# Input differences of a feed-forward made under the products ahead of it, with output blocks in the order 0 4 1 5 2 6 3 7

## Chip, cores and metric

The kernel runs on one core of a Trainium2 chip. The metric is the device time of one execution in microseconds (us). The engines are TensorE (PE, its weight loads apart as PEld), VectorE (DVE), ScalarE (ACT), GpSimd (POOL) and SyncE (SP), which issues most transfers.

## What is computed

Two layers of a decoder trunk on one sequence of 512 positions and 1024 channels, in float32. The feed-forward (FFN) width is 2816, and the mixer is a stick-breaking attention (4 heads) beside a Mamba2 scan (24 heads), both gated and merged into one output projection.

```python
def swiglu(h, w_up, w_down):
    gate, up = jnp.split(h @ w_up, 2, axis=-1)
    return (jax.nn.silu(gate) * up) @ w_down

def reference(...):
    for l in range(DEPTH):                                   # DEPTH = 2
        x = x + 0.5 * swiglu(rms_norm(x, ffn1_norm[l]), ffn1_w_up[l], ffn1_w_down[l])
        h = rms_norm(x, mix_norm[l])
        proj = h @ w_in[l]
        ...                                                  # attention, scan, their projections
        merged = jax.nn.sigmoid(gate_sb) * y_sb + jax.nn.sigmoid(gate_ssm) * y_ssm
        x = x + merged @ w_out[l]
        x = x + 0.5 * swiglu(rms_norm(x, ffn2_norm[l]), ffn2_w_up[l], ffn2_w_down[l])
    return rms_norm(x, final_norm)
```

## The kernel before

**Layout and precision.** The activations lie with channels on partitions: `x` is eight tiles of 128 channels by 512 positions, "blocks" 0 to 7. Every product is made three times with split operands (`mm3`, L291 to L293): high weight by high input, low weight by high input, high weight by low input. The high half is a copy rounded to the matmul's format, the low half the difference.

**Weight units.** The weights come as a fixed list of units of 128x1024 (`unit_order`). SP loads a unit into `wraw` (three buffers), ACT casts it to `whi` (L258), DVE subtracts to get `wlo` (L260); `ahead` starts a unit's conversion two units before its product. A dense unit is 24 matmuls of 512 columns. In the FFNs only the first blocks of gate and up are dense (`pairs_from`: four blocks in the first FFN, two elsewhere). The others go in pairs (`pair_of_blocks`): seven parts, 11, 12, s2, s1, s3, s4 and 22, each 24 matmuls of 256 columns, stand for the four dense units of two blocks. The s parts take sums of weights (`s`, by accumulating transfers from POOL's queue and an add on DVE) and, as inputs, differences of the halves of blocks k and k+4.

**Input differences.** `combine` makes them, pair after pair of blocks: two ACT copies with the gain (L354, L355), a DVE step (L357), a POOL subtraction (L358), two DVE steps (L360, L361), two ACT casts `th` (L364), and two subtractions for the low halves (L368), one on POOL and one on DVE. It starts when the FFN starts, and part s2 of the first pair needs all four. It scales by the gain alone; the norm's factor `rs` is multiplied in later, on the products.

**Norm ahead of an FFN.** As each block of `x` is finished (by the mixer's eight out products or the last slice's down products), `x_final` makes its high and low halves (`hhi` on ACT L478, `hlo` on DVE L480), its square (ACT L491) and adds that to `acc` (L498, on POOL except for block 7). `norm_end` sums over partitions with a matmul (L506) and forms `rs` (L514 to L516).

**Order.** Each engine runs its instructions in the order of the code. The code of a product calls `tick` once for each block k, and each tick lets every spawned generator (a conversion, a gate, `combine`, a norm) go one step. So an ACT or DVE step of `combine` stands among the conversions according to its ticks. FFN slices are blocks 0 to 7, 8 to 15 and 16 to 21; each ends with eight down products. The first FFN's beginning (`opening`) makes two units together as the input arrives.

Of the kernel before, what the change touches and what calls it, by code (L numbers as in the profile page):

```python
# [87 lines left out]
def pairs_from(layer, f):  # L88

    return 4 if (layer, f) == (0, 1) else 2  # L90


def unit_order(layer):

    def ffn(f):
# [29 lines left out]
    for m in range(KB):  # L125
        yield (layer, "out", m), KB
# [13 lines left out]
class Builder:  # L140
# [203 lines left out]
    def combine(self, gain):  # L344


        nc, half = self.nc, SEQ // 2
        a, b = slice(0, half), slice(half, SEQ)
        while len(self.h) < KB:
            yield 1  # L350
        for k in range(KB // 2):
            m = k + KB // 2
            u, v, x = self.tt[k], self.tt[m], self.x[k]
            nc.scalar.activation(u[:, b], x[:, b], AF.Copy, scale=gain[:, k:k + 1])  # L354
            nc.scalar.activation(v, self.x[m], AF.Copy, scale=gain[:, m:m + 1])  # L355
            yield 2
            nc.vector.scalar_tensor_tensor(u[:, a], x[:, a], gain[:, k:k + 1], u[:, b], op0=ALU.mult, op1=ALU.subtract)  # L357
            nc.gpsimd.tensor_tensor(u[:, b], v[:, b], u[:, b], op=ALU.subtract)  # L358
            yield 1
            nc.vector.scalar_tensor_tensor(v[:, b], u[:, a], -1.0, v[:, b], op0=ALU.mult, op1=ALU.subtract)  # L360
            nc.vector.scalar_tensor_tensor(v[:, a], v[:, b], -1.0, v[:, a], op0=ALU.mult, op1=ALU.subtract)  # L361
            yield 1
            for i in (k, m):
                nc.scalar.copy(self.th[i], self.tt[i])  # L364
                yield 1
            for i, eng in ((k, nc.gpsimd), (m, nc.vector)):
                lo = self.t(self.tp, [P, SEQ], "tt", F32R)
                eng.tensor_tensor(lo, self.tt[i], self.th[i].bitcast(F32), op=ALU.subtract)  # L368
                self.diff[i] = (self.th[i], lo)
            yield 1  # L370
            self.combined = k + 1
# [102 lines left out]
    def norm_split(self, m, gain):
# [6 lines left out]
        self.h.append((hi, lo))  # L481

    def norm_square(self, m, last=False):
# [13 lines left out]
        eng = nc.gpsimd if self.pos > 8 and m < KB - 1 else nc.vector  # L497
        eng.tensor_tensor(self.acc, self.acc, sq, op=ALU.add)  # L498
# [149 lines left out]
    def ffn(self, layer, f, gain, gain_next):  # L648
        tc = self.tc
        with tc.tile_pool(name=f"act{layer}{f}", bufs=8, reuse_waits="tile") as ap, \  # L650
                tc.tile_pool(name=f"ffn{layer}{f}", bufs=3, reuse_waits="tile") as fp, \
                tc.tile_pool(name=f"sx{layer}{f}", bufs=2, reuse_waits="tile") as self.sx, \
                tc.tile_pool(name=f"tt{layer}{f}", bufs=KB + 2, reuse_waits="tile") as tp:
            self.gated = {}
            self.th = [self.t(tp, [P, SEQ], "th", F32R, bufs=KB) for _ in range(KB)]
            tiles = [None] * KB
            for k in range(KB // 2):
                tiles[k], tiles[k + KB // 2] = (self.t(tp, [P, SEQ], "tt") for _ in range(2))
            self.tp, self.diff = tp, [None] * KB
            self.tt, self.combined = tiles, 0  # L660
            if self.pos:
                self.spawn(self.combine(gain))
            for s, (j0, j1) in enumerate(SLICES):
                act = []
                last = s == len(SLICES) - 1
# [19 lines left out]
                for m in range(2):  # L685
                    both.append((self.t(self.pmm, [P, SEQ], "mm"), self.unit(layer, f, "down", s, m, ahead=m == 0)))
                    self.dense(*both[m], act, 0, n - 2, stop=False)
                for m in range(KB):
                    if m < 2:
                        if m:  # L690
# [412 lines left out]
    def mixer(self, layer):  # L1103
# [13 lines left out]
        with ExitStack() as mix:  # L1117
            enter = mix.enter_context
            self.yo = enter(tc.tile_pool(name=f"yo{layer}", bufs=SBH, reuse_waits="tile"))
            self.yt = enter(tc.tile_pool(name=f"yt{layer}", bufs=24, reuse_waits="tile"))  # L1120
# [83 lines left out]

    def build(self):
# [145 lines left out]
```

## Time and profile before

| | |
|---|---|
| median of 3 runs | 2638.4 us (2638.17 to 2638.59) |
| the profiled execution's own time | 2638.81 us |
| its span in the profile | 2637.1 us |
| its mean granted TensorE clock | 0.995 |
| PE busy | 2598.7 us, 15072 matmuls |
| DVE busy | 1766.3 us, 2291 instructions |
| ACT busy | 1305.0 us, 2100 instructions |
| POOL busy | 603.3 us, 700 instructions |

Times on a timeline are counted from the span's start. A granted clock of 1 is 2.4 GHz, 0.5 is 1.2 GHz. Matmuls overlap, so a stretch of PE is measured from start to start. The four places where an FFN starts its first pair are near 57 us (layer 0's first), 990 (its second), 1339 and 2295 (layer 1's).

### The profile page before, as it was taken

How to read it: one execution, taken by the hardware profiler on the slowest of the kernel's cores; microseconds unless marked ns; L12 is line 12 of the kernel's file. 1: busy time of each engine (PE TensorE's matmuls, PEld its weight loads, DVE VectorE, ACT ScalarE, POOL GpSimd, SP SyncE). 2: the span in 40 equal slices, each digit the busy share in tenths (PEclk: the TensorE clock that was granted, in tenths of full speed). 3: DMA queues.
4: the chain of work that ended last, by engine and by line, in shares of the span. 5: the costliest groups of instructions: out<-in, count | busy, mean ns of one | idle time of the engine just before them, and what ended most of it. 6: DMA issues, size and time to landing. Idle time of an engine off the chain costs nothing.

```text
span 2637.1 us, 38181 instructions
## 1 busy us (share of the span) xinstructions
PE 2598.7 (99%) x15072; PEld 2296.3 (87%) x15072; DVE 1766.3 (67%) x2291; ACT 1305.0 (49%) x2100; POOL 603.3 (23%) x700
## 2 busy tenths in 40 slices
PE   8999999999999999999999999999999999999997
PEld 6999988888888889899988989888888888899996
DVE  7676775565665468585785858766666744785765
ACT  6443456655554245353553535566555543543444
POOL 2121211133232023021240212112332410321212
PEclk9999999999999999999999999999999999999999
DMA  5555442333333445463454644423333244374642
GB/s 177 160 144 152 119 138 74 103 105 105 115 92 127 138 136 156 135 183 112 142 141 139 168 124 133 131 75 113 96 116 104 97 136 160 89 185 130 177 123 74
DMA packets 103284, 337.94 MB, mean 128 GB/s; under 512 B 12048, under 2 KB 13328, under 8 KB 103104
## 3 DMA queue, kind: packets, MB, share of 16 engines
q1 hardware_dynamic: 91584, 294.53, 35.1%
q0 software_dynamic: 11232, 40.90, 8.7%
q8 instruction: 118, 1.93, 0.3%
q14 instruction: 62, 0.51, 0.1%
q10 hardware_dynamic: 288, 0.07, 0.0%
HBM read 322.77 MB, written 12.68 MB: 127 GB/s over the span
## 4 chain that ended last, share of the span: by engine, by line
PE 89%; DVE 6%; ACT 2%; issue 1%; POOL 1%; DMA 1%; ACTq 0%; DVEq 0%; SPq 0%; POOLq 0%
PE mm L291 25%; PE mm L293 24%; PE mm L292 24%; PE pa L293 3%; PE pa L292 3%; PE pa L291 3%; DVE wlo L260 1%; PE pa L1005 1%; PE pt L768 1%; PE pa L842 1%; PE pa L1007 1%; PE pt L990 1%; PE pt L988 1%; ACT whi L258 1%; DVE cv L906 0%
## 5 line engine op out<-in xcount | busy, mean ns | idle before, releaser
L258 ACT CAST whi<-wraw 128x1024 fp32r<-128x1024 f32 (+2 forms) x433 | 433.2, 1000 | 598.8 <-PE mm L293 497.5
L260 DVE TENSOR_TENSOR wlo<-wraw,whi 128x1024 fp32r<-128x1024 f32 (+2 forms) x433 | 572.8, 1323 | 161.4 <-ACT whi L258 160.0
L291 PE MATMUL mm<-hhi,whi 128*128 128x512 f32 (+1 forms) x1840 | 674.0, 366 | 1.9 <-ACT th L364 1.1
L292 PE MATMUL mm<-hhi,wlo 128*128 128x512 f32 (+1 forms) x1840 | 653.8, 355 | 14.5 <-DVE wlo L260 14.5
L293 PE MATMUL mm<-hlo,whi 128*128 128x512 f32 (+1 forms) x1840 | 654.7, 356 | 0.0
L292 PEld LDWEIGHTS mm<-hhi,wlo 128*128 128x128 f32 x1840 | 350.9, 191 | 59.0 <-DVE wlo L260 16.4
L293 PEld LDWEIGHTS mm<-hlo,whi 128*128 128x128 f32 x1840 | 350.2, 190 | 50.3 <-DVE hlo L480 0.3
L291 PEld LDWEIGHTS mm<-hhi,whi 128*128 128x128 f32 x1840 | 350.4, 190 | 44.0 <-ACT th L364 1.4
L601 POOL TENSOR_TENSOR g<-g,rs 128x512 f32<-128x512 f32 x78 | 137.5, 1763 | 729.8 <-DVE g L608 710.1
L260 DVE TENSOR_TENSOR wlo<-s,whi 128x1024 fp32r<-128x1024 f32 x156 | 242.1, 1568 | 53.9 <-ACT whi L258 53.9
L291 PE MATMUL mm<-act,whi 128*128 128x512 f32 x704 | 274.0, 389 | 0.0
L292 PE MATMUL mm<-act,wlo 128*128 128x512 f32 x704 | 274.0, 389 | 0.0
L293 PE MATMUL mm<-act,whi 128*128 128x512 f32 x704 | 273.9, 389 | 0.0
L292 PE MATMUL mm<-th,wlo 128*128 128x256 f32 x936 | 265.3, 283 | 1.2 <-DVE wlo L260 1.2
L291 PE MATMUL mm<-th,whi 128*128 128x256 f32 x936 | 265.1, 283 | 0.4 <-ACT g L606 0.4
L293 PE MATMUL mm<-tt,whi 128*128 128x256 f32 x936 | 265.0, 283 | 0.0
L627 DVE SCALAR_TENSOR_TENSOR x<-mm,x 128x512 f32<-128x512 f32 x96 | 66.1, 688 | 208.5 <-PE mm L293 208.5
L258 ACT CAST whi<-s 128x1024 fp32r<-128x1024 f32 x156 | 163.1, 1046 | 85.8 <-PE mm L293 46.2
L292 PEld LDWEIGHTS mm<-th,wlo 128*128 128x128 f32 x936 | 179.8, 192 | 1.8 <-DVE wlo L260 1.8
L291 PEld LDWEIGHTS mm<-th,whi 128*128 128x128 f32 x936 | 180.0, 192 | 0.6 <-ACT g L606 0.6
L293 PEld LDWEIGHTS mm<-tt,whi 128*128 128x128 f32 x936 | 179.8, 192 | 0.0
L906 DVE SCALAR_TENSOR_TENSOR cv<-mm,conv,cv 128x511 f32<-128x511 f32 (+2 forms) x192 | 142.4, 743 | 24.6 <-ACT cv L903 22.8
(258 smaller groups left out, 4630.6 us busy)
## 6 DMA issues: line engine op xcount, KB each, us to landing
wraw<-in_wflat_dram SPq DMA_DIRECT2D x353, 512.0 KB, 3.7
s<-in_wflat_dram SPq DMA_DIRECT2D x78, 512.0 KB, 5.0
s<-in_wflat_dram POOLq DMA_DIRECT2D x78, 512.0 KB, 9.1
wraw<-in_wflat_dram SPq DMA_DIRECT2D x64, 384.0 KB, 3.1
cumb<-cum_d SPq DMA_DIRECT2D x16, 768.0 KB, 4.1
xd<-x SPq DMA_DIRECT2D x16, 256.0 KB, 4.1
wraw<-in_wflat_dram SPq DMA_DIRECT2D x16, 256.0 KB, 3.3
x<-xd SPq DMA_DIRECT2D x16, 256.0 KB, 4.2
```

What stands on the lines that cost most here:

```text
L258: nc.scalar.copy(hi[:, :n], raw[:, :n])
L260: nc.vector.tensor_tensor(lo[:, :n], raw[:, :n], hi[:, :n].bitcast(F32), op=ALU.subtract)
L291: mm(ps, a[0], b[0], start=start, stop=False, **kw)
L292: mm(ps, a[1], b[0], start=False, stop=False, **kw)
L293: mm(ps, a[0], b[1], start=False, stop=stop, **kw)
L601: eng.tensor_tensor(r, r, self.rs[:, cols].unsqueeze(1).to_broadcast([P, 2, half]), op=ALU.mult)
L627: self.nc.vector.scalar_tensor_tensor(x, pd, 0.5, x, op0=ALU.mult, op1=ALU.add)
L768: self.nc.tensor.transpose(pt[:, cs], src[:, cs], self.ident)
L842: nc.tensor.matmul(pz[:, (i - j) * P:n], lhs, part, start=False, stop=(i == j and part is sps[i][1]), skip_group_check=True)
L906: nc.vector.scalar_tensor_tensor(u[:, i:], ps[:, :SEQ - i], tap[KCONV - 1 - i], u[:, i:], op0=ALU.mult, op1=ALU.add)
L988: nc.tensor.matmul(pc[:, :P], bt[:, span(c)], ct[:, span(c)], start=True, stop=True)
L990: nc.tensor.matmul(pu, btok[:, c, :], xws[c].rearrange("p h d -> p (h d)"), start=True, stop=True)
```

## The change

`combine` now makes one pair of blocks (k, k+4) and is spawned by `x_final` as soon as block k+4 has its `hlo`: during the mixer's out products for the second FFN, and during the last down products of a second FFN for the next layer's first. Out and down products go in the order 0 4 1 5 2 6 3 7. In the opening, the four are spawned 10, 19, 28 and 37 ticks after the first units. All of `combine`'s POOL steps go to DVE, and so does every `acc` addition (36 of them leave POOL). The first FFN keeps six dense blocks in place of four: one pair less. The tiles of `combine` move to a pool of their own beside `x`, which is opened with `x` at the mixer's out products; `yo` and `yt`, tiles of the mixer's branches, share that room and are closed before. Since the first out product comes behind this opening, the reloads of `x` are issued behind the mixer's last branch product.

```diff
+OUT_ORDER = tuple(i // 2 + KB // 2 * (i % 2) for i in range(KB))
...
-    return 4 if (layer, f) == (0, 1) else 2
+    return 6 if (layer, f) == (0, 1) else 2
...
-            for m in range(KB):
+            for m in OUT_ORDER:
                 yield (layer, f, "down", s, m), j1 - j0
...
-    def combine(self, gain):
...
-        while len(self.h) < KB:
-            yield 1
-        for k in range(KB // 2):
...
-            nc.gpsimd.tensor_tensor(u[:, b], v[:, b], u[:, b], op=ALU.subtract)
...
-            for i, eng in ((k, nc.gpsimd), (m, nc.vector)):
...
+    def combine(self, k, gain):
...
+        u, v = (self.t(self.tp, [P, SEQ], "uv", bufs=2) for _ in range(2))
+        nc.scalar.activation(u[:, b], x[:, b], AF.Copy, scale=gain[:, k:k + 1])
+        nc.scalar.activation(v, self.x[m], AF.Copy, scale=gain[:, m:m + 1])
+        yield 2
+        nc.vector.scalar_tensor_tensor(u[:, a], x[:, a], gain[:, k:k + 1], u[:, b], op0=ALU.mult, op1=ALU.subtract)
+        nc.vector.tensor_tensor(u[:, b], v[:, b], u[:, b], op=ALU.subtract)
+        yield 1
...
+        for t in (u, v):
+            two.append(self.t(self.tp, [P, SEQ], "th", F32R, bufs=KB))
+            nc.scalar.copy(two[-1], t)
             yield 2
...
-        eng = nc.gpsimd if self.pos > 8 and m < KB - 1 else nc.vector
-        eng.tensor_tensor(self.acc, self.acc, sq, op=ALU.add)
+        nc.vector.tensor_tensor(self.acc, self.acc, sq, op=ALU.add)
...
             yield from self.norm_split(m, gain)
+            if self.tp is not None and m >= KB // 2:
+                self.spawn(self.combine(m - KB // 2, gain), 2)
...
-            if self.pos:
-                self.spawn(self.combine(gain))
...
-                        self.spawn(self.combine(gain), 10)
+                        for k in range(KB // 2):
+                            self.spawn(self.combine(k, gain), 10 + 9 * k)
...
-            self.open_x()
...
+                branches.close()
+                self.open_x()
+                self.open_t()
+                for m in OUT_ORDER:
```

What this does to DVE's queue shows at three places. In its rows, `wlo` is the low half of a weight unit, `uv`, `th` and `tl` (before: `tt`) are `combine`'s tiles, `g`, `a` and `act` belong to the gates and `hlo` and `acc` to the norm.

The first is the opening, DVE between the low halves of two consecutive units, before:

```order
L260 TENSOR_TENSOR wlo_466<-wraw_347,whi_465 128x1024
L386 TENSOR_TENSOR act_176<-a_473,act_175 128x512
L386 TENSOR_TENSOR act_176<-a_475,act_175 128x512
L368 TENSOR_TENSOR tt_502<-tt_172,th_165 128x512
L357 SCALAR_TENSOR_TENSOR tt_173<-x_89,par_95,tt_173 128x256
L547 TENSOR_TENSOR a_519<-mm_457,g_394 128x512
L360 SCALAR_TENSOR_TENSOR tt_174<-tt_173,tt_174 128x256
L361 SCALAR_TENSOR_TENSOR tt_174<-tt_174 128x256
L386 TENSOR_TENSOR act_393<-a_519,act_392 128x512
L260 TENSOR_TENSOR wlo_522<-wraw_396,whi_521 128x1024
```

And after:

```order
L261 TENSOR_TENSOR wlo_454<-wraw_337,whi_453 128x1024
L368 TENSOR_TENSOR tl_474<-uv_410,th_450 128x512
L385 TENSOR_TENSOR act_168<-a_459,act_167 128x512
L385 TENSOR_TENSOR act_168<-a_461,act_167 128x512
L355 SCALAR_TENSOR_TENSOR uv_476<-x_88,par_106,uv_476 128x256
L356 TENSOR_TENSOR uv_476<-uv_477,uv_476 128x256
L358 SCALAR_TENSOR_TENSOR uv_477<-uv_476,uv_477 128x256
L359 SCALAR_TENSOR_TENSOR uv_477<-uv_477 128x256
L545 TENSOR_TENSOR a_511<-mm_444,g_383 128x512
L385 TENSOR_TENSOR act_382<-a_511,act_381 128x512
L261 TENSOR_TENSOR wlo_514<-wraw_385,whi_513 128x1024
```

All four 256-column steps of a `combine` now stand on DVE between these two, with one low half ahead of them; the unit that the last `wlo` belongs to is part 11 of the first pair before, and the gate of block 4 after.

The second is the start of layer 0's second FFN, DVE from the low half of part 11 to that of part 12, before:

```order
L260 TENSOR_TENSOR wlo_9121<-wraw_9002,whi_9120 128x1024
L360 SCALAR_TENSOR_TENSOR tt_8995<-tt_8994,tt_8995 128x256
L361 SCALAR_TENSOR_TENSOR tt_8995<-tt_8995 128x256
L547 TENSOR_TENSOR a_9147<-mm_9052,g_9000 128x512
L368 TENSOR_TENSOR tt_9154<-tt_8995,th_8988 128x512
L386 TENSOR_TENSOR act_8999<-a_9147,act_8998 128x512
L525 TENSOR_TENSOR g_9113<-mm_9114,rs_9086 128x512
L243 TENSOR_TENSOR s_1622_9171<-s_1593_9004,wraw_9002 128x1024
L357 SCALAR_TENSOR_TENSOR tt_8996<-x_8058,par_95,tt_8996 128x256
L360 SCALAR_TENSOR_TENSOR tt_8997<-tt_8996,tt_8997 128x256
L361 SCALAR_TENSOR_TENSOR tt_8997<-tt_8997 128x256
L260 TENSOR_TENSOR wlo_9169<-wraw_9053,whi_9168 128x1024
```

And after:

```order
L261 TENSOR_TENSOR wlo_9054<-wraw_8945,whi_9053 128x1024
L545 TENSOR_TENSOR a_9074<-mm_8995,g_8943 128x512
L385 TENSOR_TENSOR act_8942<-a_9074,act_8941 128x512
L523 TENSOR_TENSOR g_9048<-mm_9049,rs_9025 128x512
L244 TENSOR_TENSOR s_1626_9092<-s_1597_8947,wraw_8945 128x1024
L261 TENSOR_TENSOR wlo_9090<-wraw_8996,whi_9089 128x1024
```

Six steps of `combine` are gone from between the two; those of the gate and of the weight sum stay.

The third is layer 0's second FFN, DVE under the last down products, where the `combine`s of the next layer's first FFN now run. Before, two blocks:

```order
L627 SCALAR_TENSOR_TENSOR x_8056<-mm_12128,x_8056 128x512
L480 SCALAR_TENSOR_TENSOR hlo_12181<-x_8056,par_96,hhi_12180 128x512
L260 TENSOR_TENSOR wlo_12175<-wraw_12105,whi_12174 128x768
L627 SCALAR_TENSOR_TENSOR x_8057<-mm_12162,x_8057 128x512
L480 SCALAR_TENSOR_TENSOR hlo_12214<-x_8057,par_96,hhi_12213 128x512
L260 TENSOR_TENSOR wlo_12208<-wraw_12147,whi_12207 128x768
```

And after:

```order
L625 SCALAR_TENSOR_TENSOR x_8556<-mm_12039,x_8556 128x512
L479 SCALAR_TENSOR_TENSOR hlo_12092<-x_8556,par_107,hhi_12091 128x512
L261 TENSOR_TENSOR wlo_12086<-wraw_12016,whi_12085 128x768
L496 TENSOR_TENSOR acc_12081<-acc_12081,sq_12098 128x512
L355 SCALAR_TENSOR_TENSOR uv_12108<-x_8552,par_107,uv_12108 128x256
L356 TENSOR_TENSOR uv_12108<-uv_12109,uv_12108 128x256
L625 SCALAR_TENSOR_TENSOR x_8553<-mm_12073,x_8553 128x512
L358 SCALAR_TENSOR_TENSOR uv_12109<-uv_12108,uv_12109 128x256
L359 SCALAR_TENSOR_TENSOR uv_12109<-uv_12109 128x256
L479 SCALAR_TENSOR_TENSOR hlo_12133<-x_8553,par_107,hhi_12132 128x512
L261 TENSOR_TENSOR wlo_12125<-wraw_12058,whi_12124 128x768
```

`acc` and four steps of `combine` have come in between one block's `wlo` and the next block's `hlo`.

## Rows read from the trace of the kernel before

**Rows 1.** The page's busy times: engine, us (share of span), instructions.

```profile
PE 2598.7 (99%) x15072; PEld 2296.3 (87%) x15072; DVE 1766.3 (67%) x2291; ACT 1305.0 (49%) x2100; POOL 603.3 (23%) x700
```

**Rows 2.** Waits of PE: what waited for what, total us, times, longest.

```profile
PE mm L292 <- DVE wlo L260: 15.7, 9, 3.5
```

**Rows 3.** PE's timeline at pitch: start, us, instruction, [idle before <- releaser].

```profile
17.31 0.39 PE L291 MATMUL mm<-hhi,whi 128*128 128x512 f32 x1
...
22.75 0.39 PE L291 MATMUL mm<-hhi,whi 128*128 128x512 f32 x1
...
1003.32 0.28 PE L291 MATMUL pa<-th,whi 128*128 128x256 f32 x1
...
1006.20 0.28 PE L291 MATMUL mm<-th,whi 128*128 128x256 f32 x1
```

**Rows 4.** PE's timeline in the opening.

```profile
40.84 0.39 PE L293 MATMUL mm<-hlo,whi 128*128 128x512 f32 x1
...
50.72 0.50 PE L292 MATMUL mm<-hhi,wlo 128*128 128x512 f32 x1 [2.49 <-DVE wlo L260]
...
70.27 0.28 PE L291 MATMUL pa<-th,whi 128*128 128x256 f32 x1
```

**Rows 5.** PE's timeline at the first pair of the three later FFNs.

```profile
990.11 0.28 PE L291 MATMUL mm<-hhi,whi 128*128 128x256 f32 x1
...
995.66 0.39 PE L292 MATMUL mm<-hhi,wlo 128*128 128x256 f32 x1 [2.40 <-DVE wlo L260]
...
1338.94 0.28 PE L291 MATMUL mm<-hhi,whi 128*128 128x256 f32 x1
...
1346.71 0.58 PE L292 MATMUL mm<-hhi,wlo 128*128 128x256 f32 x1 [3.49 <-DVE wlo L260]
...
1354.95 0.28 PE L291 MATMUL pa<-th,whi 128*128 128x256 f32 x1
...
2294.96 0.28 PE L291 MATMUL mm<-hhi,whi 128*128 128x256 f32 x1
...
2308.16 0.28 PE L291 MATMUL pa<-th,whi 128*128 128x256 f32 x1
```

**Rows 6.** Windows: stretch, us, busy of PE, PEld, DVE, ACT, POOL, granted clock, DMA.

```profile
52.00:55.00 3.00, 3.00 (x9) 2.32 (x8) 3.00 (x5) 0.27 (x1) 1.51 (x1) 0.50 0.44 150
1347.00:1352.00 5.00, 5.00 (x24) 5.00 (x24) 4.32 (x5) 2.29 (x4) 2.48 (x2) 0.50 0.00 0
```

**Rows 7.** Timelines of ACT, DVE and POOL near 986, and two DVE steps at 40.

```profile
988.60 0.62 ACT L364 CAST th<-tt 128x512 fp32r<-128x512 f32 x1 [2.40 <-DVE tt L361]
...
985.58 1.50 DVE L360 SCALAR_TENSOR_TENSOR tt<-tt,tt 128x256 f32<-128x256 f32 x1 [0.63 <-POOL tt L358]
...
985.51 1.29 POOL L538 TENSOR_TENSOR g<-g,rs 128x512 f32<-128x512 f32 x1
...
40.06 0.69 DVE L525 TENSOR_TENSOR g<-pa,rs 128x512 f32<-128x512 f32 x1
40.66 0.41 DVE L360 SCALAR_TENSOR_TENSOR tt<-tt,tt 128x256 f32<-128x256 f32 x1
```

**Rows 8.** DVE's timeline under layer 0's last downs.

```profile
1283.48 0.95 DVE L260 TENSOR_TENSOR wlo<-wraw,whi 128x768 fp32r<-128x768 f32 x1
...
1299.33 0.75 DVE L480 SCALAR_TENSOR_TENSOR hlo<-x,par,hhi 128x512 fp32r<-128x512 f32 x1 [0.79 <-ACT hhi L478]
1300.00 2.05 DVE L260 TENSOR_TENSOR wlo<-wraw,whi 128x768 fp32r<-128x768 f32 x1
```

**Rows 9.** DVE's timeline in the opening.

```profile
35.64 1.23 DVE L260 TENSOR_TENSOR wlo<-wraw,whi 128x1024 fp32r<-128x1024 f32 x1 [1.07 <-ACT whi L258]
...
50.59 3.47 DVE L386 TENSOR_TENSOR act<-a,act 128x512 fp32r<-128x512 f32 x2
```

**Rows 10.** The page's DMA issues: transfer, queue, count, KB each, median us to landing.

```profile
s<-in_wflat_dram POOLq DMA_DIRECT2D x78, 512.0 KB, 9.1
...
x<-xd SPq DMA_DIRECT2D x16, 256.0 KB, 4.2
```

More of the change, by code (lines that the diff above doesn't have):

```diff
@@ L342, in scale_blocks @@
             yield 1
-    def combine(self, gain):
-        nc, half = self.nc, SEQ // 2
+    def combine(self, k, gain):
+        nc, half, m = self.nc, SEQ // 2, k + KB // 2
         a, b = slice(0, half), slice(half, SEQ)
-        while len(self.h) < KB:
-            yield 1
-        for k in range(KB // 2):
[L352 to L357, printed above, removed]
-            nc.gpsimd.tensor_tensor(u[:, b], v[:, b], u[:, b], op=ALU.subtract)
-            yield 1
[L360 to L365, printed above, removed]
-            for i, eng in ((k, nc.gpsimd), (m, nc.vector)):
[L367 to L371, printed above, removed]
@@ new lines, in combine @@
+        nc.vector.scalar_tensor_tensor(v[:, a], v[:, b], -1.0, v[:, a], op0=ALU.mult, op1=ALU.subtract)
+        yield 1
+        two = []
+        for t in (u, v):
+            two.append(self.t(self.tp, [P, SEQ], "th", F32R, bufs=KB))
+            nc.scalar.copy(two[-1], t)
+            yield 2
+        for i, t, hi in zip((k, m), (u, v), two):
+            lo = self.t(self.tp, [P, SEQ], "tl", F32R, bufs=KB)
+            nc.vector.tensor_tensor(lo, t, hi.bitcast(F32), op=ALU.subtract)
+            self.diff[i] = (hi, lo)
+            yield 1
@@ L684, in ffn @@
                 n, both = j1 - j0, []
-                for m in range(2):
+                for m in OUT_ORDER[:2]:
                     both.append((self.t(self.pmm, [P, SEQ], "mm"), self.unit(layer, f, "down", s, m, ahead=m == 0)))
[L687 to L690, printed above, removed]
+                    self.dense(*both[-1], act, 0, n - 2, stop=False)
+                for i, m in enumerate(OUT_ORDER):
+                    if i < 2:
+                        if i:
                             self.ahead(1)
-                        ps = both[m][0]
-                        self.dense(*both[m], act, n - 2, n, start=False, base=0)
+                        ps = both[i][0]
+                        self.dense(*both[i], act, n - 2, n, start=False, base=0)
                     else:
@@ L1191, in mixer @@
                 gain = self.pars[layer][:, G_FFN2:G_FFN2 + KB]
-                for m in range(KB):
+                branches.close()
+                self.open_x()
+                self.open_t()
+                for m in OUT_ORDER:
                     nc.sync.dma_start(self.x[m], xd[m])
@@ L1203, in open_x, with open_t, close_t @@
         self.x = [self.t(xp, [P, SEQ], "x") for _ in range(KB)]
+    def open_t(self):
+        self.tpool = self.tc.tile_pool(name=self.name("tpool"), bufs=2, side="right", reuse_waits="tile")
+        self.tp = self.tpool.__enter__()
+    def close_t(self):
+        self.tpool.__exit__(None, None, None)
+        self.tp = None
     def build(self):
@@ L1216, in build @@
         self.open_x()
+        self.open_t()
+        self.tt = [self.t(self.tp, [P, SEQ], "tl", bufs=KB) for _ in range(KB)]
         nc.scalar.preload_act_table_set("natural_log_exp_and_others")
```

34 lines of the change are left out of this document (17 added, 17 removed).

## The prediction

> **What bounds the kernel now.** I read the busy shares first: TensorE (PE) is busy for 2598.7 of 2637.1 us [rows 1], so the end moves only if matmuls are added or dropped, if PE waits less or more, or if its clock changes. Next the waits of PE. The largest entry by far is a matmul that needs a weight's low half, `wlo`, which VectorE (DVE) makes at L260: nine waits, 15.7 us in all [rows 2]. Then I read PE's timeline where these waits lie. They are not spread over the kernel; they sit where each feed-forward turns from dense units to its first pair of blocks.
>
> To price such a stretch I need the undisturbed pitch. A dense unit is 24 matmuls of 512 columns and took 22.75 − 17.31 = 5.44 us, 0.2267 each; a part of a pair is 24 of 256 columns and took 1006.20 − 1003.32 = 2.88 us, 0.12 each [rows 3]. What a stretch took beyond pitch is what can be recovered there:
> - Opening, 40.84 to 70.27 [rows 4]: 29.43 − 49 × 0.2267 − 72 × 0.12 = 9.7 us.
> - Layer 0's second FFN, 990.11 to 1003.32 [rows 5, 3]: 13.21 − 72 × 0.12 = 4.6.
> - Layer 1's first FFN, 1338.94 to 1354.95 [rows 5]: 16.01 − 72 × 0.12 = 7.4.
> - Layer 1's second FFN, 2294.96 to 2308.16 [rows 5]: 13.20 − 72 × 0.12 = 4.6.
>
> (The 72 are the parts 11, 12 and s2 of the first pair, 24 matmuls each.) Together 26.3 us, by the unrounded terms 26.2. Part of it is clock: behind the 2.49 us wait at 50.72 and the 3.49 us wait at 1346.71 TensorE ran at a granted 0.50, that is 1.2 GHz, for 3 to 5 us [rows 6]. After the 2.40 us wait at 995.66 it did not fall: that stretch is at pitch from 1003.32 on.
>
> Why is `wlo` late there? ScalarE (ACT) and DVE run in the order of the code. In layer 0's second FFN the ACT copy `th` of the third block pair's differences stood 2.40 us until DVE's L361 was done; the cast `whi` behind it, and the subtraction `wlo` behind that, came late by as much, and PE took the product up at 995.66, after 2.40 us [rows 7, 5]. DVE's 256-column step at 985.58 took 1.50 us while POOL's 1.29 us multiplication ran, against 0.41 alone at 40.66 [rows 7]. So the chain of `combine`, through ACT, DVE, POOL and DVE, stands between the weights' conversions.
>
> **The change, part by part.** *Differences made earlier.* In three of four stages the four `combine`s now run under the mixer's out products or the FFN's last down products; behind them only `wlo` and the gates' steps are left in DVE's queue. In the opening they are spaced by 9 ticks and share the time with four more dense units of 5.44 us. The stalls named above lose their cause: −26.2 us, if nothing takes their place. Lower bound of this gain: the opening's share and none of the other three, −9.7.
>
> *The new cover.* Under a down product (18 matmuls, 4.08 us) DVE did `x`, `hlo`, `wlo` and stood 0.79 us for ACT's `hhi` [rows 8]. `wlo` took 2.05 us beside POOL's `acc`, 0.95 without [rows 8]. With POOL's `acc` moved to DVE a product costs DVE, from start to start, about 0.60 + 0.67 + 0.87 + 0.60 (`acc`, a 512-column step: 40.06 to 40.66 [rows 7]), and half a `combine`: four steps of some 0.42 and two of 0.60, half of 2.9 = 1.45. That is 4.2 against a pitch of 4.08: DVE is full. The wait for `hhi` is mostly filled with `combine` steps, since they stand between `x` and `hlo` in the new order. Eight products lag by 8 × 0.12 = 1 us at most; weights are made two units ahead (8.2 us), so PE doesn't see it, but the last block's `hlo`, needed by layer 1's first gate, does: I take +0.6 us. Bounds: 0 when the lag dissolves, and 8 × 0.79 = 6.3 when no wait is filled. Under the mixer's out products the pitch is 5.44 and the same sum, with 0.25 more for a wider `wlo`, is about 4.5: free.
>
> A rule speaks against moving POOL's work to DVE. The Trainium skill, "Perfetto Trace Analysis", section "Optimizing Scalar/DVE Operations", says that a saturated DVE may be relieved by moving work to ScalarE or GpSimd, though between those two it might not help as they share a port; this change loads the fuller engine. The rows bear out the port rather than the relief: 2.05 against 0.95 for one `wlo` is 1.1 us lost, while `acc` on DVE costs 0.60.
>
> *One pair fewer.* In the first FFN blocks 4 and 5 become dense: 4 × 24 × 0.2267 = 21.76 us in place of 7 × 24 × 0.12 = 20.16. +1.6 us, rounded with its edges to +1.7.
>
> *Opening.* This is the one place where I expect a new wait. The `wlo` at 35.64 waited 1.07 us for a cast that stood behind `combine`'s copies in ACT's queue [rows 9]; I put its end at 35.4, about 1.3 us earlier than now. From there to the `wlo` of the fifth gate unit, DVE now has 14 steps of 512 columns (three of the rs chain, three g, three `a`, three `act`, two `lo`) at 0.60, eight of 256 columns (two `combine`s) at 0.43, and two `wlo` at 1.14 and 1.22: 14.2 us, and 0.8 for steps that wait for the one before, 15.0. PE would want that `wlo` two units and a matmul after the one that ends at 40.84 + 0.23, at 41.07 + 10.88 + 0.23 = 52.2 [rows 4]; 35.4 + 15.0 = 50.4 would do. But three POOL multiplications by rs fall there, and DVE is held while they run: two `act` steps took 3.47 us at 50.59 instead of about 1.4 [rows 9]. By some 1.05 us for each of three, and about 1.3 for ACT's copies, it becomes some 54.5 to 54.9: a wait of 2.3 to 2.7, of which I take +2.2, since the three POOL steps hardly all fall on two-input steps. Bounds: 0 when POOL doesn't get in the way, and 2.7 + 1.6 when the clock also falls for 3 us as at 52 to 55 [rows 6], at half speed 1.5 lost: 4.3.
>
> The hold is what the Trainium skill, "SBUF — State Buffer", section "Who interferes with whom", describes as an exclusive lock on a shared port pair; this case's rows agree in kind (1.50 against 0.41, 2.05 against 0.95).
>
> *Moved loads.* SP's reload of `x` waits now for the last branch product instead of an earlier step; three products of 5.44 us lie between it and the first out product, so about 16 us cover a load of 4.2 us [rows 10]. The accumulating load of the first pair's weight sums takes 9.1 us from POOL's queue [rows 10] and is now freed by the last out product, four dense units (21.8 us) ahead of its pair, of which two loads in a row need some 18. Nothing, or up to 4 us if the two queue up badly: in the range only.
>
> *Order of blocks, pools.* The order 0 4 1 5 … changes no duration. The tail after the last matmul hangs on block 7 either way: 0.
>
> **Sum.** −26.2 + 0.6 + 1.7 + 2.2 = −21.7 us. The profiled execution took 2638.81 us, so it would become 2617.1; the median of the runs lay 0.4 lower, so the forecast is 2616.7.
>
> **Rivals.**
> - *A, clean opening* (chance 0.16). POOL's multiplications fall between DVE's two-input steps and no wait appears: −23.9, so 2614.5 for the median. For it: 50.4 is before 52.2. Against: rows 9.
> - *B, a worse opening or more lag* (0.18). The new wait draws a stretch at 1.2 GHz (+1.6), or the last `hlo` or the weight sums are some us late (+2 to +6): 2619 to 2623.
> - *C, the later stalls are not `combine`'s* (0.09). The first pair has its own load: weight sums on DVE and conversions two units ahead of parts of 2.88 us. If that sets the waits, 4.6 + 7.4 + 4.6 = 16.6 us stay: 2616.7 + 16.6 = 2633.3, on the edge of no change. For it: in each of the three stages the long wait is on `wlo` of part 12. Against: the ACT queue at 988.60 shows `combine` right ahead of it.
> - *D, slower: DVE becomes the bound under the last downs* (0.07). If `wlo` keeps 2.05 us without POOL's `acc` (because ACT, not POOL, slows it), a product costs DVE 0.60 + 0.67 + 1.97 + 0.60 + 1.45 = 5.3 against 4.08: 8 × 1.2 = 9.6 us, all of which the first gate of layer 1 waits for; the same slow `wlo` keeps the 16.6 us and doubles the opening's wait to 4.4, and a stretch at 1.2 GHz follows (2.5). 2638.4 − 26.2 + 16.6 + 1.7 + 9.6 + 4.4 + 2.5 = 2647.0. It decides from 5.1 us of DVE work for a product (4.08 plus an eighth of the 8.2 us ahead). Against: `wlo` took 0.95 at 1283.48 with POOL idle.
>
> **How the numbers follow.** My forecast has 0.50, A 0.16, B 0.18, C 0.09, D 0.07. A measurement of this kernel can tell about 0.2% (5.3 us) from no change, so faster means below 2633.1: forecast, A, B and a third of C, 0.87; same: most of C, and a D without its slow clock, 0.08; slower: 0.05. The range runs from just below A, 2612, to the upper end of B with its bounds, 2625; C and D lie outside.
>
> **What the new profile would show.** The parts 11 and 12 of the three later stages at 2.88 us each with no wait on `wlo` above 0.5 us; `wlo` under the last downs at about 0.95; DVE's `acc` at 0.6 to 0.7 there; PE's first gate of layer 1's first FFN waiting on `hlo` for about 0.6; one wait of some 2 us on `wlo` at the fifth gate of the opening. I am wrong if a wait over 2 us stands at any of the three later first pairs, if the granted clock falls there again, or if PE waits inside the out or down products.

## The result and the profile after

The median went from 2638.67 us (2638.17 to 2639.64) to 2617.11 us (2616.44 to 2617.70), six runs each; the ratio is 0.9918, 95% interval 0.9905 to 0.9931. The forecast was 2616.7. The profiled execution took 2617.70 us, with a span of 2615.8.

Where the time went is read from landmarks that both kernels have: the norm's matmul over partitions, once for each norm. On PE's timeline of the kernel after (start, us, instruction) they are these:

```profile
28.61 1.13 PE L504 MATMUL pt<-acc,ones 128*128 128x512 f32 x2
...
364.19 1.02 PE L504 MATMUL pt<-acc,ones 128*128 128x512 f32 x2
...
968.53 1.02 PE L504 MATMUL pt<-acc,ones 128*128 128x512 f32 x2
...
1314.27 1.12 PE L504 MATMUL pt<-acc,ones 128*128 128x512 f32 x2
...
1658.35 1.02 PE L504 MATMUL pt<-acc,ones 128*128 128x512 f32 x2
...
2262.87 1.02 PE L504 MATMUL pt<-acc,ones 128*128 128x512 f32 x2
...
2600.08 1.02 PE L504 MATMUL pt<-acc,ones 128*128 128x512 f32 x2
```

In the trace of before they start at 27.83, 369.77, 974.25, 1322.98, 1674.62, 2279.09 and 2620.87. The differences give the time of each stage. A stage ends just behind the first gate unit of the next one, so a wait at that gate counts to the stage ahead of it.

| stretch | before | after | change |
|---|---|---|---|
| start to the first norm | 27.83 | 28.61 | +0.8 |
| layer 0, first FFN | 341.94 | 335.58 | −6.4 |
| layer 0, mixer | 604.48 | 604.34 | −0.1 |
| layer 0, second FFN | 348.73 | 345.74 | −3.0 |
| layer 1, first FFN | 351.64 | 344.08 | −7.6 |
| layer 1, mixer | 604.47 | 604.52 | 0.0 |
| layer 1, second FFN | 341.78 | 337.21 | −4.6 |
| the rest | 16.2 | 15.7 | −0.5 |

All of it lies in the FFNs. The waits of PE (what waited for what, total us, times, longest) say the same against [rows 2]: 15.7 us in nine waits for `wlo` became 2.1 in two (one of them, 0.57, ahead of the first norm, where before has 0.56), and one of 1.1 for `hhi` is new.

```profile
PE mm L293 <- DVE wlo L261: 2.1, 2, 1.6
...
PE mm L292 <- ACT hhi L477: 1.1, 1, 1.1
```

The first pair of layer 0's second FFN, on PE's timeline of after, answers to [rows 5]:

```profile
984.40 0.28 PE L292 MATMUL mm<-hhi,whi 128*128 128x256 f32 x1
...
993.03 0.28 PE L292 MATMUL pa<-th,whi 128*128 128x256 f32 x1
```

Parts 11, 12 and s2 took 8.63 us, 72 matmuls at the pitch of 0.12, where they had taken 13.21. In layer 1's FFNs they took 8.63 as well (1330.21 to 1338.84, 2278.73 to 2287.36), for 16.01 and 13.20. The granted clock answers to [rows 6]; the windows (stretch, us, busy of PE, PEld, DVE, ACT, POOL, clock, DMA) cover the opening's new wait and layer 1's first pair:

```profile
54.50:60.00 5.50, 5.31 (x23) 4.42 (x24) 4.94 (x10) 4.08 (x7) 0.13 (x1) 1.00 0.35 99
...
1329.00:1338.00 9.00, 9.00 (x72) 8.77 (x71) 6.92 (x8) 4.15 (x5) 1.32 (x2) 1.00 0.26 81
```

Two waits are new. Here is PE at the fifth gate of the opening (the matmul before it started at 52.72, so 1.97 − 0.23 = 1.74 us were lost), and then at the first gate of layer 1 (1.46 − 0.23 = 1.23 lost), both in after:

```profile
54.69 0.50 PE L293 MATMUL mm<-hhi,wlo 128*128 128x512 f32 x1 [1.58 <-DVE wlo L261]
...
1310.29 0.39 PE L294 MATMUL mm<-hlo,whi 128*128 128x512 f32 x1
1311.75 0.50 PE L292 MATMUL mm<-hhi,whi 128*128 128x512 f32 x1 [1.06 <-ACT hhi L477]
```

### The profile page after: what moved, and what is told of

Its sections match the earlier page's. It is cut to its first block, busy times and chain, and to the rows that moved or that the text cites. A ratio compares the mean times of both kernels' runs of the same rounds, so it can differ in the third digit from the quotient of the medians.

```text
span 2615.8 us, 38022 instructions
## 1 busy us (share of the span) xinstructions
PE 2592.5 (99%) x15000; PEld 2289.3 (88%) x15000; DVE 1750.1 (67%) x2352; ACT 1299.0 (50%) x2094; POOL 508.9 (19%) x629
## 4 chain that ended last, share of the span: by engine, by line
PE 93%; DVE 4%; ACT 1%; DMA 1%; issue 1%; POOL 0%; SPq 0%; DVEq 0%; ACTq 0%
PE mm L292 26%; PE mm L294 26%; PE mm L293 26%; PE pa L293 3%; PE pa L294 3%; PE pa L292 3%; PE pa L999 1%; PE pt L762 1%; PE pa L836 1%; DVE wlo L261 1%; PE pa L1001 1%; PE pt L984 1%; PE pt L982 1%; DVE cv L900 0%; ACT whi L259 0%
## 5 line engine op out<-in xcount | busy, mean ns | idle before, releaser
L261 DVE TENSOR_TENSOR wlo<-wraw,whi 128x1024 fp32r<-128x1024 f32 (+2 forms) x434 | 542.3, 1250 | 168.2 <-ACT whi L259 166.3
L261 DVE TENSOR_TENSOR wlo<-s,whi 128x1024 fp32r<-128x1024 f32 x152 | 235.5, 1563 | 58.2 <-ACT whi L259 58.2
L292 PE MATMUL mm<-th,whi 128*128 128x256 f32 x912 | 258.1, 283 | 0.0
L293 PE MATMUL mm<-th,wlo 128*128 128x256 f32 x912 | 258.1, 283 | 0.0
L294 PE MATMUL mm<-tl,whi 128*128 128x256 f32 x912 | 258.1, 283 | 0.0
L294 PEld LDWEIGHTS mm<-tl,whi 128*128 128x128 f32 x912 | 175.1, 192 | 0.0
```

The source lines that it names most:

```text
L261: nc.vector.tensor_tensor(lo[:, :n], raw[:, :n], hi[:, :n].bitcast(F32), op=ALU.subtract)
L292: mm(ps, a[0], b[0], start=start, stop=False, **kw)
L293: mm(ps, a[1], b[0], start=False, stop=False, **kw)
L294: mm(ps, a[0], b[1], start=False, stop=stop, **kw)
```

## The experiments

My theory was that the place of `combine`, in the engines' queues ahead of the weights' conversions, made the waits; that POOL's steps added to it by holding DVE; and that the opening needs the time of the extra dense units. Its rivals: POOL alone was the trouble, the first pair's own load was, or some part does nothing. The table gives for each run the median, and the stages' times by the same landmarks of its trace (L0F1 is layer 0's first FFN; the mixers are left out where they stay within 0.2 us of 604.4). L0F1 is good to some 1.5 us only: e2 has the opening of after, but its first norm comes 1.7 us earlier, and L0F1 is 1.6 us longer, in longer waits of the opening.

| kernel | median us | L0F1 | L0F2 | L1F1 | L1F2 |
|---|---|---|---|---|---|
| before | 2638.2 to 2638.7 | 341.94 | 348.73 | 351.64 | 341.78 |
| after | 2617.11 | 335.58 | 345.74 | 344.08 | 337.21 |
| e1, before, POOL's steps on DVE | 2632.22 | 339.40 | 348.45 | 348.44 | 340.14 |
| e2, after, combines at the FFN's start | 2630.24 | 337.19 | 349.04 | 349.10 | 340.75 |
| e3, after, `acc` on POOL | 2621.25 | 335.72 | 348.75 | 344.26 | 337.25 |
| e4, after, `acc` and `combine` on POOL | 2619.94 | 336.98 | 347.12 | 344.26 | 337.21 |
| e5, after, four dense blocks | 2623.02 | 340.42 | 345.76 | 344.11 | 337.21 |
| e6, after, natural order | 2620.38 | 335.75 | 346.24 | 344.12 | 337.29 |
| e7, after, opening spaced | 2615.37 | 333.72 | 345.75 | 344.10 | 337.22 |
| e8, after, `combine` on POOL | 2620.48 | 338.30 | 347.73 | 344.47 | 337.22 |
| e9, after, spaced and held | 2614.22 | 333.70 | 344.23 | 345.09 | 337.21 |
| e10, before, six dense blocks | 2639.04 | 342.24 | 348.71 | 351.55 | 342.07 |

### Place or engine: e1 and e2

e1 takes the kernel before and changes engines only:

```diff
-            nc.gpsimd.tensor_tensor(u[:, b], v[:, b], u[:, b], op=ALU.subtract)
+            nc.vector.tensor_tensor(u[:, b], v[:, b], u[:, b], op=ALU.subtract)
...
-            for i, eng in ((k, nc.gpsimd), (m, nc.vector)):
+            for i, eng in ((k, nc.vector), (m, nc.vector)):
...
-        eng = nc.gpsimd if self.pos > 8 and m < KB - 1 else nc.vector
-        eng.tensor_tensor(self.acc, self.acc, sq, op=ALU.add)
+        nc.vector.tensor_tensor(self.acc, self.acc, sq, op=ALU.add)
```

> The kernel before with its POOL steps of combine and its acc additions on DVE, nothing moved in time and the blocks in natural order. Theory (the place of combine among the conversions makes the stalls): the chain still stands ahead of whi and wlo at each first pair, only its steps are shorter (0.42 for 1.50 us) and the hops to POOL are gone, so 2 to 10 of the 26 us go: 2628 to 2636 us, and PE still waits over 1 us on wlo at the first pairs. Rival (POOL, slow and in DVE's way, makes the stalls, wherever combine stands): some 20 us go, 2618 us, no long wait on wlo left.

It gave 2632.22 us, a ratio of 0.9975 (0.9965 to 0.9984): 6 of the 21 us. Its waits of PE:

```profile
PE mm L292 <- DVE wlo L260: 8.5, 8, 2.1
PE mm L291 <- ACT g L605: 3.0, 3, 1.0
```

Half of the wait for `wlo` is left, and each of the three later first pairs now has one of 1.0 us for ACT's copy of `g`. In layer 0's second FFN that copy comes at 993.83 behind an `act` cast, which stood 2.35 us for DVE's `a`, and that step stood behind the two last subtractions of `combine` on DVE. These took 2.38 us, beside POOL's multiplication of a gate by `rs` at 989.58, which e1 leaves where it was. So taking the steps of `combine` and `acc` off POOL isn't enough.

e2 takes the kernel after and moves the combines of the three later FFNs back to the FFN's start, at the old pace:

```diff
+    def combine_all(self, gain):
+        while None in self.h:
+            yield 1
+        for k in range(KB // 2):
+            yield from self.combine(k, gain)
...
+            if self.pos:
+                self.spawn(self.combine_all(gain))
...
-            if self.tp is not None and m >= KB // 2:
-                self.spawn(self.combine(m - KB // 2, gain), 2)
...
             nc.scalar.copy(two[-1], t)
-            yield 2
+            yield 1
...
-            yield 1
+        yield 1
```

> The kernel after with the four combines of the three later FFNs started where the FFN starts, one behind the other at the pace of before; everything on DVE, order of blocks, opening as in after. Theory: the stalls at the three later first pairs return, 8 to 17 us of the 16.6, less about 1.5 us because the end of the last downs is lighter: 2624 to 2633 us, with waits of PE on wlo near parts 11 and 12. Rival (the move off POOL is what helped): 2615 to 2617 us, no such wait.

It gave 2630.24 us, 13 more than after. The three stages lost 3.3, 5.0 and 3.5 us, and L0F2 had gained 1.5 of its own, since layer 1's first gate has no wait there. So about 13 of the 16.6 us come back with the place. Some 3 of the 13 are clock: in two of the three FFNs the granted clock fell behind the waits (0.67 over 994.00 to 997.00, for one). The other 3 or so go with what e2 keeps of the change, above all DVE's steps in place of POOL's; e1, which has only those, is 5.1 us shorter than before in the same three stages. How the place makes the wait shows in the first pair of layer 0's second FFN in e2, ACT's timeline and then DVE's:

```profile
986.15 0.62 ACT L364 CAST th<-uv 128x512 fp32r<-128x512 f32 x1 [1.59 <-DVE uv L356]
...
987.72 1.04 ACT L259 CAST whi<-s 128x1024 fp32r<-128x1024 f32 x1
...
985.12 0.47 DVE L355 SCALAR_TENSOR_TENSOR uv<-x,par,uv 128x256 f32<-128x256 f32 x1
985.70 0.42 DVE L356 TENSOR_TENSOR uv<-uv,uv 128x256 f32<-128x256 f32 x1
986.16 0.43 DVE L358 SCALAR_TENSOR_TENSOR uv<-uv,uv 128x256 f32<-128x256 f32 x1
986.62 0.43 DVE L359 SCALAR_TENSOR_TENSOR uv<-uv 128x256 f32<-128x256 f32 x1
986.96 1.22 DVE L261 TENSOR_TENSOR wlo<-wraw,whi 128x1024 fp32r<-128x1024 f32 x1
```

No POOL step is among them and every DVE step has its short duration. Still ACT stood 1.59 us for DVE's L356, with the next conversion's cast queued behind, and DVE put four steps ahead of `wlo`, whose own cast had ended at 984.57; PE waits 0.75 us for that `wlo` at 988.23, so DVE's queue alone makes this wait.

It accounts for the first of the pair's three waits only. The other two, for ACT's copy of `g` and for the `wlo` of part s2, come behind `combine`'s last two subtractions; here are DVE, POOL and PE in e2:

```profile
988.10 2.38 DVE L368 TENSOR_TENSOR tl<-uv,th 128x512 fp32r<-128x512 f32 x2
...
987.39 1.94 POOL L542 TENSOR_TENSOR g<-g,rs 128x512 f32<-128x512 f32 x1 [6.45 <-ACT g L540]
...
992.26 0.38 PE L292 MATMUL mm<-th,whi 128*128 128x256 f32 x1 [1.01 <-ACT g L610]
993.64 0.39 PE L293 MATMUL mm<-th,wlo 128*128 128x256 f32 x1 [0.99 <-DVE wlo L261]
```

Two such subtractions took 1.28 us at 981.58, where POOL stood idle. So place and contention work together in these two waits: the multiplications by `rs` stay on POOL in every run, and what they hold depends on what stands beside them on DVE. No run takes them off POOL, so their own share isn't shown.

The rival that the first pair's own load makes the waits is excluded by the kernel after itself, which makes the same weight sums and casts at pitch.

### What POOL's steps cost: e3, e4 and e8

e3 is the kernel after with `acc` back on POOL (the last two lines of e1's diff reversed). e8 has `combine`'s two POOL steps back instead (the other lines reversed), and e4 has both.

> The kernel after with the 36 acc additions on POOL again. Theory (a POOL step holds a two-input step of DVE for its whole time): under layer 0's last downs wlo takes about 2.0 us for 0.95, a product costs DVE 4.7 us against a pitch of 4.08, the lag grows by up to 8 x 0.6 = 5 us and the first gate of layer 1 waits 3 to 6 us longer; the mixers' out products (5.0 of 5.44) stay covered: 2620 to 2622 us. Rival (DVE is the fuller engine, so POOL relieves it): about 1 us faster, 2616 us, and the wait at that gate shrinks.

It gave 2621.25 us, 4.1 more than after. Under layer 0's last downs, DVE's timeline in e3 and then POOL's:

```profile
1301.42 1.78 DVE L368 TENSOR_TENSOR tl<-uv,th 128x512 fp32r<-128x512 f32 x1
...
1305.26 2.31 DVE L261 TENSOR_TENSOR wlo<-wraw,whi 128x1024 fp32r<-128x1024 f32 x1
...
1300.97 1.68 POOL L497 TENSOR_TENSOR acc<-acc,sq 128x512 f32<-128x512 f32 x1 [4.22 <-ACT sq L490]
1305.16 1.34 POOL L497 TENSOR_TENSOR acc<-acc,sq 128x512 f32<-128x512 f32 x1 [2.51 <-ACT sq L490]
```

Each `acc` holds whatever two-input step DVE has then: 1.78 us for a `tl` of 0.68, 2.31 for a `wlo` of 1.22. That is 1.1 us to save 0.6. L0F2 became 3.0 us longer. I had called the mixers' out products covered; they became 0.8 and 0.6 us longer (605.15 and 605.11), so they aren't quite.

> The kernel after with acc and combine's two POOL steps on POOL as in before, combines still early. Theory: on top of the run with acc alone on POOL, each combine takes 1.0 us of steps off DVE but holds it for some 1.5 to 2 us: another +1 to +3 us at layer 1's first gate and some more in the opening: 2621 to 2625 us. Rival (relief): 2615 us.

It gave 2619.94 us, 1.3 less than e3, against the theory's sign: with `acc` on POOL already, `combine` on POOL as well was better under the downs (L0F2 347.12 for 348.75), though worse in the opening (+1.3).

> The kernel after with combine's two POOL steps (the subtraction and one low half) on POOL as before, acc left on DVE. From the runs with acc alone and with everything on POOL (2621.3 and 2619.9): theory A (a POOL step pays when it takes as much off DVE as it holds DVE, and combine's steps fall beside one-input or short steps): 1 us off the 1.66 us of waiting at layer 1's first gate, some tenths lost in the opening: 2616 us. Theory B (every step moved to POOL holds DVE longer than it would take there): 1 to 2 us slower than after, 2618 to 2619 us.

With `acc` on DVE the same move cost 3.4 us: 2620.48 (the five executions lie between 2618.6 and 2622.7), theory B and more. In the trace 2.7 are in L0F1, of which 1.7 is a stretch at 1.2 GHz behind the fifth gate (the last section shows it), and 2.0 in L0F2. DVE in e8's opening, and POOL behind it:

```profile
39.58 1.50 DVE L358 SCALAR_TENSOR_TENSOR uv<-uv,uv 128x256 f32<-128x256 f32 x1 [0.91 <-POOL uv L356]
41.11 1.39 DVE L359 SCALAR_TENSOR_TENSOR uv<-uv 128x256 f32<-128x256 f32 x1
...
39.50 2.72 POOL L536 TENSOR_TENSOR g<-g,rs 128x512 f32<-128x512 f32 x2
```

The hop to POOL costs 0.91 us of waiting and puts the next two steps beside POOL's multiplications. So the parts don't add up: each of e3 and e8 alone is worse than after, by 4.1 and 3.4, and both together by 2.8. I have no run that says why. The kernel with all of these steps on DVE is the fastest of the four.

### The opening: e5, e7 and e10

```diff
-    return 6 if (layer, f) == (0, 1) else 2
+    return 4 if (layer, f) == (0, 1) else 2
...
-                            self.spawn(self.combine(k, gain), 10 + 9 * k)
+                            self.spawn(self.combine(k, gain), 10 + 8 * k)
```

> The kernel after with four dense blocks in the first FFN as in before (one more pair), the opening's combines 8 ticks apart instead of 9. Theory (the opening's conversions need the time of the four extra dense units): 1.6 us of matmuls fewer, but the four combines now share six units instead of ten with the conversions, and their steps stand ahead of parts 11, 12 and s2; the opening's excess over pitch goes from 1.9 us in after back to 5 to 8 of the 9.7 us in before: 2619 to 2622 us. Rival (the extra dense blocks bring nothing, only the cost of their columns): 2615.5 us.

It gave 2623.02 us (2621.7 to 2625.1), just above the theory's range; L0F1 went to 340.42, 4.8 more than after. PE in e5 met `wlo` late at parts 11 and 12; the first of the two waits on its timeline, and the window behind it, with the clock at 1.2 GHz:

```profile
55.57 0.58 PE L293 MATMUL mm<-hhi,wlo 128*128 128x256 f32 x1 [3.00 <-DVE wlo L261]
...
55.40:58.40 3.00, 2.83 (x13) 2.83 (x14) 2.90 (x7) 1.64 (x3) 0.00 (x0) 0.50 0.02 5
```

The second wait, behind the matmul that started at 60.64, cost another 1.7 us. e10 is the opposite: the kernel before with six dense blocks.

> The kernel before with six dense blocks in the first FFN and nothing else changed. Theory (combine's place at the conversions makes the stalls): the three later FFNs keep their 16.6 us; in the opening the two waits at dense units stay (about 1.2 and 2.6 us and the slow clock behind them) and those at parts 11 and 12 (1.9 and 1.6) go, against 1.6 us for the wider columns: 2636 to 2638 us. Rival (the extra dense blocks alone gave the opening its gain of 7.8 - 1.7 us): 2632 us.

It gave 2639.04 us, a ratio of 1.0001 (0.9992 to 1.0010): nothing, and neither theory's time. The waits only changed their unit, and where I expected 1.9 + 1.6 us to go, a wait of 3.27 us came at a dense unit, behind the matmul that started at 55.32, with 1.2 GHz behind it. No run spreads the combines and changes nothing else. e5 has them spread and POOL's steps on DVE, and takes 1.5 us off L0F1, while POOL's steps alone take 2.5 (e1): spreading without the time of the extra dense units shows no gain. Six dense blocks alone lose 0.3. Both together with POOL's steps left as in before, which is e4, take 5.0 off, and with POOL's steps moved too, 6.4. So the wider columns cost 1.6 us and buy time in which the spread combines fit.

e7 spreads them further:

```diff
-                            self.spawn(self.combine(k, gain), 10 + 9 * k)
+                            self.spawn(self.combine(k, gain), 10 + 16 * k)
```

> The kernel after with the opening's combines 16 ticks apart instead of 9. Theory (the wait of 1.74 us at the fifth gate is DVE holding two combines between two conversions): the wait goes and none takes its place, since 64 ticks still end before the first pair: 2615.3 us, 1.8 faster than after. Rival (the wait is POOL's rs multiplications, or only moves to a later unit): 2617 us, the same 1.7 us of waits on wlo in the opening.

It gave 2615.37 us, and L0F1 333.72, 1.9 less than after: the new wait is gone and none took its place.

### Order of blocks: e6

```diff
-OUT_ORDER = tuple(i // 2 + KB // 2 * (i % 2) for i in range(KB))
+OUT_ORDER = tuple(range(KB))
...
-        u, v = (self.t(self.tp, [P, SEQ], "uv", bufs=2) for _ in range(2))
+        u, v = (self.t(self.tp, [P, SEQ], "uv", bufs=4) for _ in range(2))
```

> The kernel after with out and down products in the order 0 to 7, so that the combines start with blocks 4 to 7; the combine tiles uv get four buffers since two combines overlap. Theory (DVE is full under the last four products): a down product costs DVE 0.60+0.67+0.87+0.60+2.9 = 5.6 us for 4.08, an out product 6.0 for 5.44; the last block comes 6 us later at layer 1's first gate and 1 to 2 us later at the two second FFNs: 2622 to 2628 us, PE waiting at the gates' starts on hhi or hlo. Rival (it matters only that the combines are done before the first pair; four dense units hide them in any order): 2617 us.

It gave 2620.38 us, 3.3 more than after. The mixers became 1.0 and 0.9 us longer (605.38, 605.40) and L0F2 0.5; the direction is the theory's, the size is about half of it, below its range. I had counted the last four products alone; DVE is ahead of PE when they begin, since the first four carry no combine.

### A faster version: e9

e9 has e7's spacing and holds the later two combines until block 7 is through:

```diff
-                self.spawn(self.combine(m - KB // 2, gain), 2)
+                self.spawn(self.combine(m - KB // 2, gain), 2 if m < 6 else 12)
```

> The kernel after with the opening's combines 16 ticks apart and, at the norms, the combines of blocks 2 and 3 held 12 ticks instead of 2, so that two of the four run under the next FFN's first dense units. Theory (layer 1's first gate waits because DVE's lag under the last downs delays block 7): with one combine of 2.9 us less ahead of block 7 the wait of 1.2 to 1.7 us there goes, on top of the 1.75 of the opening: 2613.9 us. Rival (DVE has no room under the dense units either): the wait moves to wlo of parts 11 and 12, 1 us or more at each of three FFNs, 2616 to 2619 us.

It gave 2614.22 us, ratio 0.9908 (0.9892 to 0.9925), and is the fastest of these kernels. L0F2 lost another 1.5 us, the whole wait at layer 1's first gate; 1.0 came back in L1F1, where PE waits 0.50 at 1329.68 for the `wlo` of part 12. So the rival holds, at half its size, for one of the three FFNs, and half a microsecond is still open there. PE's waits on `wlo` in e9 (the one of 0.6 lies ahead of the first norm), and the `wlo` of part 12 with POOL beside it:

```profile
PE mm L293 <- DVE wlo L261: 1.1, 2, 0.6
...
1327.30 2.32 DVE L261 TENSOR_TENSOR wlo<-wraw,whi 128x1024 fp32r<-128x1024 f32 x1
...
1327.00 1.54 POOL L536 TENSOR_TENSOR g<-g,rs 128x512 f32<-128x512 f32 x1 [3.88 <-ACT g L534]
```

This `wlo` took 2.32 us for 1.22, again beside POOL's multiplication by `rs`: that hold is larger than the wait that is left.

## Why the prediction was right

- **What bounds the kernel.** Right. Each of the four stretches that had been priced beyond pitch is where the time went. The three later ones lost their whole excess (8.63 us for 72 matmuls, three times), so −26.2 as the gain's gross size held. e2 shows that the place made 13 of the 16.6 us of these three, and e1 that `combine`'s and `acc`'s steps on POOL were worth 6 us in all. Two of the prediction's readings fell short. In layer 1's second FFN part of the 4.6 was clock as well: behind the wait at 2300.49 the windows of before show 0.50 granted over 2302.00 to 2304.00. And `wlo` for the wait at 995.66 was not late because `whi` was: its cast ended at 991.74, and `wlo` stood in DVE's own queue until 994.39, behind the next pair's steps, which waited for POOL's L358. ACT and DVE in before:

```profile
990.70 1.04 ACT L258 CAST whi<-wraw 128x1024 fp32r<-128x1024 f32 x1
...
993.59 0.42 DVE L360 SCALAR_TENSOR_TENSOR tt<-tt,tt 128x256 f32<-128x256 f32 x1 [0.91 <-POOL tt L358]
...
994.39 1.22 DVE L260 TENSOR_TENSOR wlo<-wraw,whi 128x1024 fp32r<-128x1024 f32 x1
```

  `combine` stands in the way either way, as the prediction says, but through DVE's queue here and not through ACT's.
- **One pair fewer, +1.7.** L0F1 changed by −6.4 = −9.7 + 1.85 (the new wait, 1.74, and 0.11 behind it) + p, so p, the cost of the wider columns, is +1.5.
- **The new wait in the opening, +2.2.** Right in place (the fifth gate) and nearly in size, 1.85. Its make-up was partly wrong. DVE in after, with POOL behind it:

```profile
40.15 1.33 DVE L356 TENSOR_TENSOR uv<-uv,uv 128x256 f32<-128x256 f32 x1
...
42.91 0.68 DVE L545 TENSOR_TENSOR a<-pa,g 128x512 f32<-128x512 f32 x1
44.07 0.69 DVE L545 TENSOR_TENSOR a<-mm,g 128x512 f32<-128x512 f32 x1 [0.48 <-POOL g L536]
...
48.80 1.33 DVE L356 TENSOR_TENSOR uv<-uv,uv 128x256 f32<-128x256 f32 x1
...
52.81 0.69 DVE L385 TENSOR_TENSOR act<-a,act 128x512 fp32r<-128x512 f32 x1 [1.16 <-ACT act L380]
...
39.80 1.39 POOL L536 TENSOR_TENSOR g<-g,rs 128x512 f32<-128x512 f32 x1 [38.17 <-ACT g L534]
...
42.74 1.30 POOL L536 TENSOR_TENSOR g<-g,rs 128x512 f32<-128x512 f32 x1 [1.55 <-ACT g L534]
...
48.52 1.34 POOL L536 TENSOR_TENSOR g<-g,rs 128x512 f32<-128x512 f32 x1 [4.48 <-ACT g L534]
```

  Two of the three multiplications held a step, by 0.9 us each, not three by 1.05. The one at 42.74 held nothing: the step at 42.91 reads one input from PSUM (`pa`) and took its 0.68; but the next `a`, at 44.07, needs its result and waited 0.48. The 1.16 us for ACT stands for the 1.3 that I had put down. With the 15.0 us of counted steps that makes 18.4; from the end of the first `wlo` (36.28) to that of the fifth gate's (54.64) it was 18.36. Both the start and the moment when PE wants the fifth gate's `wlo` (52.95 for 52.2) came 0.8 to 0.9 us later than I had put them, which cancels.
- **The last block's `hlo`, +0.6.** The term that was mis-sized: the wait at layer 1's first gate grew by 1.55 us (1.23, and 0.43 in the next three matmuls, against 0.11 in before), and it is for `hhi` (ACT stood 1.26 us for DVE's `x` of block 7, which was late), where I had named `hlo`. DVE's `hlo` of blocks 4, 5, 6 and 7 in after:

```profile
1284.93 0.75 DVE L479 SCALAR_TENSOR_TENSOR hlo<-x,par,hhi 128x512 fp32r<-128x512 f32 x1 [1.07 <-ACT hhi L477]
...
1293.68 0.75 DVE L479 SCALAR_TENSOR_TENSOR hlo<-x,par,hhi 128x512 fp32r<-128x512 f32 x1 [0.20 <-ACT hhi L477]
...
1302.44 0.75 DVE L479 SCALAR_TENSOR_TENSOR hlo<-x,par,hhi 128x512 fp32r<-128x512 f32 x1 [0.19 <-ACT hhi L477]
...
1311.73 0.75 DVE L479 SCALAR_TENSOR_TENSOR hlo<-x,par,hhi 128x512 fp32r<-128x512 f32 x1 [0.20 <-ACT hhi L477]
```

  They come 8.75, 8.76 and 9.29 us apart, for two products at 4.08 each: 4.4 to 4.65 us of DVE a product, where the sum said 4.2. It left out the 0.2 us that the wait for `hhi` keeps, and that the last two `wlo` ahead of block 7's `hlo` belong to 1024-wide gate units (1.22 us for 0.95).
- **`wlo` without POOL's `acc`.** Right: 0.95 under the downs, `acc` 0.68 on DVE, and e3 shows the price of the other way, so rival D's condition, that ACT and not POOL slowed `wlo`, is false. The rule of the Trainium skill ("Perfetto Trace Analysis", section "Optimizing Scalar/DVE Operations") that moving work between DVE and GpSimd might not help is borne out by e3, which makes that move: 0.6 us of `acc` taken off DVE cost it 1.1.
- **Loads and pools, 0.** Nothing waits there: the mixers kept their time within 0.2 us.
- **Outside the sum**: 0.8 us more up to the first norm and 0.5 less behind the last. The former varies by itself: that landmark lies between 26.87 and 28.61 in these twelve traces.
- **The total.** 2617.1 was forecast for the profiled execution, which took 2617.70. The terms were off by more than that: +0.95 on the last block's `hlo`, −0.35 on the opening's wait, −0.2 on the wider columns, +0.3 outside the sum. That they nearly cancel is luck.

## What to carry to other kernels

A chain that crosses in-order engines cost time here only where something urgent was queued behind it; find the cast or subtraction that stands there, price the stretch by what it took beyond pitch, and move the chain to where its steps fall beside work with slack. When the new place is full, count the steps of the engine per product against the pitch, waits for the other engine included, and spread them; e9 took 2.9 us more by spacing and holding back alone. Changes made together may pay only together, as the extra dense blocks and the spread combines do here, so each should be undone and also made alone.

## What the runs showed of the hardware

The clock's fall isn't told by the length of the wait alone. In e4 a wait of 2.39 us for `wlo` in the opening was followed by full clock; in e8 one of 2.40 us at the same gate was followed by 1.2 GHz. PE's row and a window behind it of e4, then of e8 (the last number but two is the clock; in e4 it stays at 1.00 to 64.00):

```profile
55.29 0.50 PE L293 MATMUL mm<-hhi,wlo 128*128 128x512 f32 x1 [2.39 <-DVE wlo L261]
...
57.00:58.00 1.00, 1.00 (x6) 0.83 (x5) 0.46 (x2) 0.49 (x1) 1.00 (x2) 1.00 0.79 303
```

```profile
54.04 0.50 PE L293 MATMUL mm<-hhi,wlo 128*128 128x512 f32 x1 [2.40 <-DVE wlo L261]
...
56.00:58.00 2.00, 2.00 (x6) 1.52 (x6) 1.61 (x4) 1.76 (x3) 2.00 (x3) 0.50 0.51 129
```

In the kernel before the same shows within one trace: behind 2.40 us at 995.66 the clock stayed at 1.00 (996.00 to 999.00), behind 2.38 us at 2300.49 it was 0.50 (2302.00 to 2304.00).

A DVE step with one input in PSUM ran beside POOL undisturbed (0.68 us at 42.91 above), while one with two SBUF inputs was held for most of POOL's step (1.33 for 0.42). The Trainium skill, "SBUF — State Buffer", section "Who interferes with whom", says the same: a DVE instruction with at most one SBUF input, outside the 2-port perf modes, does not contend with GpSimd. Of the three multiplications that the prediction counted in the opening, two met a step with two SBUF inputs and one a step with one.
